# Layer 1's keys and queries: token sums behind the root, scaling by VectorE from one slot, values behind their pair, weight sums last

## The chip, the cores and the metric

One core of one Trainium2 chip runs the whole program in a single launch. TensorE (PE in the profile, PEld for its weight loads) does the matrix products, VectorE (DVE), ScalarE (ACT) and GpSimd (POOL) the elementwise work, SyncE (SP) and POOL issue most transfers. The metric is the device time of one execution in microseconds. A change of less than 0.2% (2.4 us) can't be told from no change here.

## The reference, cut to what matters

Two layers over 512 tokens of width 1024, in float32. Layer 0 has two kinds of dense attention, layer 1 has a neighbourhood attention with 16 heads of 64 columns. Each layer ends in a squared-ReLU MLP. The change touches layer 1's attention only.

```
def rmsnorm(x, g):
    y = xf * lax.rsqrt(jnp.mean(xf * xf, axis=-1, keepdims=True) + EPS)
    return (y * g.astype(jnp.float32)).astype(x.dtype)

def neighbourhood_attention(h, w_qkv, rpb, w_out):
    q, k, v = jnp.split(h @ w_qkv, 3, axis=-1)
    ...
        kg = jnp.take(k, iblk, axis=2)
        vg = jnp.take(v, iblk, axis=2)
        bias = rpb[:, rblk, cblk].astype(jnp.float32)
        sc = jnp.einsum('bhqd,bhqkd->bhqk', qblk, kg).astype(jnp.float32) * scale + bias[None]
        p = jax.nn.softmax(sc, axis=-1).astype(vg.dtype)
        return jnp.einsum('bhqk,bhqkd->bhqd', p, vg)
    ...
    return o @ w_out

for layer in range(DEPTH):
    hn = rmsnorm(h, norm_mix[layer])
    ...
        h = h + neighbourhood_attention(hn, od_w_qkv[i], od_rpb[i], od_w_out[i])
    h = h + sq_relu_mlp(rmsnorm(h, norm_ffn[layer]), ffn_w_up[layer], ffn_w_down[layer])
```

## The kernel before

**Numbers in two parts.** Every float32 operand of a product is split into a high part (ACT rounds it to fp32r) and a low part (DVE takes the difference). A product is three matmuls: high by high, high by low, low by high. `whi` and `wlo` are the parts of a weight chunk; `a` names the 8 KB slots that hold tokens, keys, queries and values, `sc` scratch tiles, `mm`, `s`, `t` and `o` the eight banks of PSUM (products, scores, transposes, outputs).

**The root.** The norm's factor of a token is the reciprocal root of its sum of squares. PE sums the squares (L661), DVE takes the mean and, in ten small operations, the root (L663, L186 to L196), and copies it to `r` (L1635). PE spreads it over 128 partitions (L669, a broadcast and transpose), ACT puts it into `rb` (L1641). The products run on tokens without the factor; it is multiplied in when keys and queries are evacuated from PSUM, and for values by L1863 and L1864.

**Keys and queries in pairs of heads.** Eight pairs, t = 0 to 7. `projC(t)` is the plain form: 48 matmuls of 128x128 by 128x512, keys first, then queries. The key's evacuation (L1687) and the query's (L1720, two pieces with a factor 0.125) multiply by `rb` on DVE. `projC7(t)`, for t = 1 to 5, is a seven-block form: the 2x2 blocks of weights and tokens are combined so that seven products do for eight, 84 matmuls of 128x128 by 128x256. It needs sums of weight blocks and of token blocks. `seven_pair` loads a chunk of weights and lets POOL make its sums (L390 to L392), then splits it (L396, L397). `SevenC.sums(kp)` makes the token sums for chunk pair kp = 0 to 3: ACT scales two chunks (L1661), POOL combines them (L1664 to L1666), ACT and DVE split the results (L1671, L1672). Four banks take a pair's products. `ev` combines them: ACT copies a half bank (L1771), DVE adds in four operations (L1774 to L1780), POOL multiplies by `rb` in five (L1781 to L1786), ACT and DVE split. The parts must also lie in the other half of the partitions: two transfers by POOL's queue (L1810, L1811) and, behind L1811's landing, one by SP's (L1815) for a query.

**The attention.** `attend_C` goes through 16 heads in two half-steps each: scores (L1898, four matmuls), DVE's bias and minimum (L1913), transposes of the head before (L1924), the exponential (L1932), the normalisation by POOL (L1902), and the output of the head before that (L1944). Between them the queue `fill` runs matmuls of projections not done yet: before this change, for t = 1 to 7, `projC7(t)` or `projC(t)`, with the values of four heads (`valuesC`, L1845 to L1847) put ahead of pairs 2, 4 and 6, and from head 12 on a part of the output projection. `RATE_C` sets how much is run at each place; `fill.until` makes a head wait until its pair was issued.

**What sets the order.** Inside the attention PE, ACT, DVE and POOL issue in the order in which the code is written (`fixed_order`); SP's is scheduled. Work that could hold up an engine is not written at once: `soon` puts it into the list `off_d`, `soon_a` into `off_a`, and `catch_up` takes it at fixed places. `banks_for` releases the PSUM layout and opens another: in `psC` five banks for products and one each for s, t and o, in `psD` three, two, two and one. Ahead of the attention a scheduler orders the instructions, except those that are pinned by `keep_in_program_order`.

## Time and profile before

| | us |
|---|---|
| runs | 1199.89, 1200.42, 1202.01; median 1200.42 |
| profiled execution | 1200.05, of which span 1198.30 |
| PE, DVE, ACT, POOL busy | 1150.9 (96%), 928.8 (78%), 688.5 (57%), 669.4 (56%) |
| before the attention's stage | to 600 |
| layer 1's attention with its opening | 600 to 842 |
| output projection's rest, MLP, final norm | 842 to 1198.3 |

The page's first part gives busy times. Since PE is nearly always busy, the views to read are those of its waits: by cause (`PE s L1898 <- DMA a<-sc` is PE's scores at line 1898 waiting for a transfer from scratch into a slot), by stretch (the windows, with the clock that PE was granted, 1.00 being full speed), and the timeline of an engine, where a bracket gives the idle time before an instruction and what ended it.

### The profile page before, as it was taken

Reading aid. Unit: us, or ns where it says so; the run is one execution under the profiler, and the core shown is the slowest. Engines: PE = TensorE matmul, PEld = TensorE weight load, DVE = VectorE, ACT = ScalarE, POOL = GpSimd, SP = SyncE. Lnnn points to the kernel's source line nnn. Section 1 sums busy time; section 2 is a strip of 40 time slices with the busy share of each in tenths; the row PEclk is TensorE's granted clock in tenths of the full one; section 3 lists DMA queues with packets and bytes.
Section 4 is the critical chain, followed back from the end, with each engine's and each line's share of the span. In section 5 each row is a group of like instructions: output and inputs, shape, how many; then the busy total and the mean of one; then the engine's idle time right before and its main releaser. Section 6 shows DMA issues by size and latency. Waiting matters only on the chain. (4 is left out here: it accounts for less than half of the span.)

```text
span 1198.3 us, 21112 instructions
## 1 busy us (share of the span) xinstructions
PE 1150.9 (96%) x7528; PEld 1037.1 (87%) x7528; DVE 928.8 (78%) x1593; ACT 688.5 (57%) x1164; POOL 669.4 (56%) x819
## 2 busy tenths in 40 slices
PE   9999999999999999999959797998999999999997
PEld 8787888888899998999949797877888999989996
DVE  7888998798778879787786765765798788688884
ACT  6576875656266677344745554644562566774434
POOL 4366422237888862697657854320087888626640
PEclk9999999999999999999979899999999999999999
DMA  7322441123422329434824535543335233182332
GB/s 228 106 82 69 106 124 54 47 95 117 153 76 87 106 69 264 156 106 128 155 70 111 147 109 142 136 120 114 97 98 166 72 93 102 56 196 67 116 130 71
DMA packets 118329, 136.10 MB, mean 114 GB/s; under 512 B 9923, under 2 KB 99952, under 8 KB 118224
## 3 DMA queue, kind: packets, MB, share of 16 engines
q1 hardware_dynamic: 110736, 119.83, 33.2%
q0 software_dynamic: 7312, 14.83, 6.6%
q8 instruction: 59, 0.97, 0.3%
q14 instruction: 46, 0.38, 0.1%
q10 hardware_dynamic: 176, 0.10, 0.0%
HBM read 112.70 MB, written 6.29 MB: 99 GB/s over the span
## 5 line engine op out<-in xcount | busy, mean ns | idle before, releaser
L376 DVE TENSOR_TENSOR wlo<-a,whi 128x896 fp32r<-128x896 f32 x106 | 132.6, 1253 | 56.7 <-ACT whi L375 56.2
L375 ACT ACTIVATE whi<-a 128x896 fp32r<-128x896 f32 x106 | 100.8, 951 | 111.6 <-PE o L479 28.6
L478 PE MATMUL mm<-a,whi 128*128 128x256 f32 x570 | 161.7, 284 | 2.8 <-DVE sc L1720 1.6
L480 PE MATMUL mm<-a,wlo 128*128 128x256 f32 x570 | 160.2, 281 | 4.1 <-DVE wlo L397 4.0
L479 PE MATMUL mm<-a,whi 128*128 128x256 f32 x570 | 159.8, 280 | 0.0
L640 PE MATMUL mm<-a,whi 128*128 128x512 f32 x348 | 142.8, 411 | 1.7 <-DVE sc L1117 1.7
L642 PE MATMUL mm<-a,wlo 128*128 128x512 f32 x348 | 138.5, 399 | 1.7 <-DVE wlo L229 1.7
L641 PE MATMUL mm<-a,whi 128*128 128x512 f32 x348 | 138.6, 398 | 0.0
L229 DVE TENSOR_TENSOR wlo<-raw,whi 128x1024 fp32r<-128x1024 f32 (+4 forms) x83 | 93.9, 1137 | 31.2 <-ACT whi L239 30.9
L239 ACT ACTIVATE whi<-raw 128x1024 fp32r<-128x1024 f32 (+3 forms) x86 | 77.4, 903 | 59.6 <-PE s L641 30.1
L480 PEld LDWEIGHTS mm<-a,wlo 128*128 128x128 f32 x570 | 107.5, 189 | 4.8 <-DVE wlo L397 4.7
L478 PEld LDWEIGHTS mm<-a,whi 128*128 128x128 f32 x570 | 107.6, 189 | 4.0 <-ACT whi L396 2.0
L479 PEld LDWEIGHTS mm<-a,whi 128*128 128x128 f32 x570 | 107.6, 189 | 0.1
L371 POOL TENSOR_TENSOR a<-a 128x128 f32<-128x128 f32 x104 | 100.9, 970 | 8.2
L375 ACT ACTIVATE whi<-raw 128x896 fp32r<-128x896 f32 x58 | 55.2, 954 | 83.7 <-POOL raw L371 24.9
L1173 POOL TENSOR_SCALAR p<-p,ti 128x512 f32<-128x512 f32 x64 | 47.3, 740 | 89.9 <-DVE ti L1172 66.6
L370 POOL TENSOR_TENSOR a<-a 128x256 f32<-128x256 f32 x104 | 92.5, 890 | 8.2
L376 DVE TENSOR_TENSOR wlo<-raw,whi 128x896 fp32r<-128x896 f32 x58 | 72.1, 1258 | 21.6 <-ACT whi L375 21.5
L478 PE MATMUL t<-a,whi 128*128 128x256 f32 x312 | 87.5, 281 | 0.0
L480 PE MATMUL t<-a,wlo 128*128 128x256 f32 x312 | 87.4, 280 | 0.0
L479 PE MATMUL t<-a,whi 128*128 128x256 f32 x312 | 87.3, 280 | 0.0
L369 POOL TENSOR_TENSOR a<-a 128x128 f32<-128x128 f32 x104 | 66.1, 636 | 34.5 <-DMA a<-in_ffn_w_up_dram 20.4
(477 smaller groups left out, 3688.2 us busy)
## 6 DMA issues: line engine op xcount, KB each, us to landing
a<-in_ffn_w_up_dram SPq DMA_DIRECT2D x102, 256.0 KB, 2.7
raw<-in_ffn_w_down_dram SPq DMA_DIRECT2D x34, 512.0 KB, 4.2
raw<-in_ffn_w_down_dram SPq DMA_DIRECT2D x56, 256.0 KB, 2.6
raw<-in_od_w_qkv_dram SPq DMA_DIRECT2D x64, 128.0 KB, 2.7
raw<-in_ffn_w_up_dram SPq DMA_DIRECT2D x12, 512.0 KB, 4.2
wlo<-in_ffn_w_down_dram POOLq DMA_DIRECT2D x12, 512.0 KB, 6.2
a<-a SPq DMA_DIRECT2D x17, 256.0 KB, 3.2
bx<-a SPq DMA_DIRECT2D x32, 128.0 KB, 5.4
```

The lines of the kernel that those rows point to most:

```text
L229: z = lambda: (eng or DVE).tensor_tensor(to, src, f32(high), op=ALU.subtract)
L239: ACT.activation(hi[:, 0:m], raw[:, 0:m], AF.Copy)
L370: held(eng.tensor_tensor(r[:, 4:6], r[:, 2:3].to_broadcast([P, 2, P]), r[:, 0:7:6], op=ALU.add))
L371: held(eng.tensor_tensor(r[:, 7], r[:, 3], r[:, 5], op=ALU.subtract))
L375: ACT.activation(hi[:, 0:896], raw[:, 128:1024], AF.Copy)
L376: DVE.tensor_tensor(lo[:, 0:896], raw[:, 128:1024], f32(hi[:, 0:896]), op=ALU.subtract)
L478: PE.matmul(o, wh, x[:, 0], start=kp == 0 and n in (0, 1, 3, 5), stop=False, skip_group_check=True)
L479: PE.matmul(o, wh, x[:, 1], start=False, stop=False, skip_group_check=True)
L480: PE.matmul(o, wl, x[:, 0], start=False, stop=kp == self.np - 1, skip_group_check=True)
L640: PE.matmul(o, wh, xh, start=first, stop=False)
L641: PE.matmul(o, wh, xl, start=False, stop=False)
L642: PE.matmul(o, wl, xh, start=False, stop=last)
```

## The change

1. The token sums were written between pair 0's products; now they are written behind them, all four in turn, and their first ACT operations (L1661) are pinned.
2. Pair 1 takes the plain form; the seven-block form is left for pairs 2 to 5.
3. `ev` of the seven-block form works in one slot instead of three scratches, and DVE does the scaling: one multiplication for keys, two with 0.125 for queries, in place of POOL's five.
4. POOL's weight sums of a chunk go into a list of their own, taken behind the normalisations of a half-step, or when the chunk is needed.
5. The values stand behind pairs 2, 4 and 6 in `fill` and no longer ahead of them.
6. The `psD` layout is opened inside the attention, by an entry of `fill` behind pair 5, and not after it.
7. `RATE_C` goes from 1.26 to 1.28.

```diff
--- before.py
+++ after.py
@@ -323,7 +323,7 @@
 
 
 
-    off_d, off_a = [], []
+    off_d, off_a, off_p = [], [], []
 
     def soon(z, later=None):
         if fixed[0]:
@@ -387,10 +387,16 @@
                          src[:, 0:2, P * t : P * t + P])
         r = raw.rearrange("p (b n) -> p b n", n=P)
         yield
-        POOL.tensor_tensor(r[:, 6], r[:, 0], r[:, 1], op=ALU.subtract)
-        POOL.tensor_tensor(r[:, 4:6], r[:, 2:3].to_broadcast([P, 2, P]), r[:, 0:7:6], op=ALU.add)
-        POOL.tensor_tensor(r[:, 7], r[:, 3], r[:, 5], op=ALU.subtract)
+
+        def sums():
+            POOL.tensor_tensor(r[:, 6], r[:, 0], r[:, 1], op=ALU.subtract)
+            POOL.tensor_tensor(r[:, 4:6], r[:, 2:3].to_broadcast([P, 2, P]), r[:, 0:7:6], op=ALU.add)
+            POOL.tensor_tensor(r[:, 7], r[:, 3], r[:, 5], op=ALU.subtract)
+
+        soon(sums, off_p)
         yield
+        while sums in off_p:
+            off_p.pop(0)()
         hi = wp.tile([P, 1024], F32R, tag="whi", name=nm("whi"))
         lo = wp.tile([P, 1024], F32R, tag="wlo", bufs=4, name=nm("wlo"))
         ACT.activation(hi[:, 0:896], raw[:, 128:1024], AF.Copy)
@@ -1658,7 +1664,8 @@
 
             raw, t = Slot(F32), scratch()
             for z in range(2):
-                ACT.activation(raw.t[:, S * z : S * z + S], hT[:, 2 * kp + z, :], AF.Copy, scale=gmix(1, 2 * kp + z))
+                tc.keep_in_program_order(ACT.activation(raw.t[:, S * z : S * z + S], hT[:, 2 * kp + z, :], AF.Copy,
+                                                        scale=gmix(1, 2 * kp + z)))
             yield
             r, t_ = (x.rearrange("p (b n) -> p b n", n=256) for x in (raw.t, t))
             POOL.tensor_tensor(t_, r[:, 0:1].to_broadcast([P, 2, 256]), r[:, 1:3], op=ALU.subtract)
@@ -1765,25 +1772,26 @@
 
         def ev(bk, half):
             d = PC[t]
-            X, Y, nq, nk = (scratch() for _ in range(4))
+            w_, rb = Slot(F32), hold["rb"]
+            n_, nk = scratch(), scratch()
+            r = w_.t.rearrange("p (b n) -> p b n", n=256)
             two = lambda b: b.rearrange("p (b n) -> p b n", n=256)
-            rb = hold["rb"]
-            ACT.activation(Y[:, 0:256], half(bk[0], 0), AF.Copy)
+            ACT.activation(r[:, 1], half(bk[0], 0), AF.Copy)
 
             def first():
-                DVE.tensor_tensor(two(X), two(Y)[:, 0:1].to_broadcast([P, 2, 256]), two(bk[1]), op=ALU.add)
-                DVE.tensor_tensor(two(Y), two(X)[:, 0:1].to_broadcast([P, 2, 256]), two(bk[2]), op=ALU.add)
+                DVE.tensor_tensor(r[:, 0:4:3], r[:, 1:2].to_broadcast([P, 2, 256]), two(bk[1]), op=ALU.add)
+                DVE.tensor_tensor(r[:, 1:3], r[:, 0:1].to_broadcast([P, 2, 256]), two(bk[2]), op=ALU.add)
                 soon(second)
 
             def second():
-                DVE.tensor_tensor(X[:, 0:256], Y[:, 0:256], half(bk[2], 1), op=ALU.add)
-                DVE.tensor_tensor(Y, Y, bk[3], op=ALU.add)
-                POOL.tensor_tensor(nk[:, 0:256], Y[:, 256:512], rb[:, 0:256], op=ALU.mult)
-                POOL.tensor_tensor(nk[:, 256:512], X[:, 256:512], rb[:, 256:512], op=ALU.mult)
+                DVE.tensor_tensor(r[:, 0], r[:, 1], half(bk[2], 1), op=ALU.add)
+                DVE.tensor_tensor(r[:, 1:3], r[:, 1:3], two(bk[3]), op=ALU.add)
+                DVE.tensor_tensor(nk, w_.t[:, S : 2 * S], rb, op=ALU.mult)
                 soon_a(lambda: split(nk, ka, down))
-                POOL.tensor_tensor(nq[:, 64:320], X[:, 0:256], rb[:, 0:256], op=ALU.mult)
-                POOL.tensor_tensor(nq[:, 320:512], Y[:, 0:192], rb[:, 256:448], op=ALU.mult)
-                POOL.tensor_tensor(nq[:, 0:64], Y[:, 192:256], rb[:, 448:512], op=ALU.mult)
+                for to, fr, m in ((64, 0, 448), (0, 448, 64)):
+                    DVE.scalar_tensor_tensor(n_[:, to : to + m], w_.t[:, fr : fr + m], 0.125, rb[:, fr : fr + m],
+                                             op0=ALU.mult, op1=ALU.mult)
+                w_.free()
                 soon_a(high)
 
             d["K"] = [Slot(), Slot()]
@@ -1802,11 +1810,11 @@
             lo = scratch(F32R)
 
             def high():
-                ACT.activation(q[:, 0, :], nq, AF.Copy, scale=0.125)
+                ACT.activation(q[:, 0, :], n_, AF.Copy)
                 soon(low)
 
             def low():
-                DVE.scalar_tensor_tensor(lo, nq, 0.125, f32(q[:, 0, :]), op0=ALU.mult, op1=ALU.subtract)
+                DVE.tensor_tensor(lo, n_, f32(q[:, 0, :]), op=ALU.subtract)
                 POOL.dma_start(f32(q[0:64, 1, :]), f32(q[64:128, 0, :]))
                 POOL.dma_start(f32(q[64:128, 1, :]), f32(lo[64:128, :]))
                 soon(last)
@@ -1961,6 +1969,7 @@
             for x in w:
                 norm(*x)
             catch_up()
+            take_up(off_p)
             fill.run(us)
             catch_up()
 
@@ -2012,25 +2021,29 @@
     next(root)
     for _ in first:
         pass
-    parts = [xC.sums(kp) for kp in range(4)]
     for n, _ in enumerate(second):
         if n == 2:
             next(root)
-        if n % 2 == 1:
-            for kp in range(4):
-                if kp <= n // 2 < kp + 3:
-                    next(parts[kp])
-    for x in parts:
-        for _ in x:
+    for kp in range(4):
+        for _ in xC.sums(kp):
             pass
+
+    def new_banks(name, **bufs):
+        finish_off()
+        banks_for(name, **bufs)
+        return
+        yield
+
     for t in range(1, 8):
+        fill.add(f"c{t}", projC7(t) if 2 <= t < 6 else projC(t))
+        if t == 5:
+            fill.add("c5", new_banks("psD", mm=3, s=2, t=2, o=1))
         if t in (2, 4, 6):
-            fill.add(f"c{t}", valuesC(t // 2, lambda: [mmb(), mmb()]))
-        fill.add(f"c{t}", projC7(t) if t < 6 else projC(t))
+            fill.add(f"v{t}", valuesC(t // 2, lambda: [mmb(), mmb()]))
     w_out1 = ins["od_w_out"][0]
     okC = [None] * 5
     rest = [out_proj(w_out1, 0, okC, cols, "out") for cols in ([0, 1, 2], [3, 4, 5], [6, 7])]
-    LEAD, RATE_C = 11.0, 1.26
+    LEAD, RATE_C = 11.0, 1.28
 
     def step(n):
         if n == 14:
@@ -2050,7 +2063,6 @@
         attend_C(step)
         give_low(len(ready))
         fixed[0] = 0
-    banks_for("psD", mm=3, s=2, t=2, o=1)
     ok = [s_.pair() for s_ in O[5:]]
     flip[0] = 1
     for c in range(2):
```

The order of the instructions shows what that does. Lines of the changed kernel are 6 to 8 higher for the same code (L1661 is L1667 there, L1671 is L1678, L1672 is L1679, L1687 is L1694).

ACT at the opening, before: the token sums (`a<-hT,gT` is the scaling of a chunk) stand ahead of the values' scaling by the root, L1863.

```order
L1661 ACTIVATE a_7153<-hT,gT 128x512
L1671 ACTIVATE a_7163<-sc_7134 128x2x256
L1671 ACTIVATE a_7166<-a_7133 128x2x256
L1661 ACTIVATE a_7172<-hT,gT 128x512 x2
L1671 ACTIVATE a_7182<-sc_7154 128x2x256
L1671 ACTIVATE a_7185<-a_7153 128x2x256
L1661 ACTIVATE a_7191<-hT,gT 128x512 x2
L1671 ACTIVATE a_7211<-sc_7173 128x2x256
L1671 ACTIVATE a_7214<-a_7172 128x2x256
L396 ACTIVATE whi_7279<-raw_7251 128x896
L1863 ACTIVATE a_7093<-o_6944,r_7061 128x4x64
```

The same place after: L1737 and L1738 are the split of pair 0's query (L1730 and L1731 before), and each chunk pair's scaling stands behind the split of the one before it.

```order
L1737 ACTIVATE sc_7184<-sc_7180 64x512
L1738 ACTIVATE a_7183<-sc_7180 64x512
L1667 ACTIVATE a_7191<-hT,gT 128x512 x2
L1678 ACTIVATE a_7198<-sc_7192 128x2x256
L1678 ACTIVATE a_7201<-a_7191 128x2x256
L1667 ACTIVATE a_7204<-hT,gT 128x512 x2
L402 ACTIVATE whi_7318<-raw_7265 128x896
L1678 ACTIVATE a_7211<-sc_7205 128x2x256
L1678 ACTIVATE a_7214<-a_7204 128x2x256
L1667 ACTIVATE a_7217<-hT,gT 128x512 x2
```

The sums moved from ahead of the root to behind pair 0's query, and the scaling no longer runs one chunk pair ahead.

DVE after, in the third and fourth chunk pair's sums (L1679): L1921 is the first head's scores, L1694 and L1727 pair 1's key and query.

```order
L1679 TENSOR_TENSOR a_7224<-sc_7218,a_7224 128x2x256
L1679 TENSOR_TENSOR a_7227<-a_7217,a_7227 128x2x256
L1921 ISA p_7360,ti_7365<-s_7359,bias_7357 128x256
L1921 ISA ti_7365 128x1
L1921 ISA p_7360,ti_7367<-s_7359,bias_7357 128x256
L1921 ISA ti_7367 128x1
L1694 TENSOR_TENSOR sc_7334<-mm_7248,rb 128x512
L1727 SCALAR_TENSOR_TENSOR sc_7371<-mm_7247,rb 128x448
L1727 SCALAR_TENSOR_TENSOR sc_7371<-mm_7247,rb 128x64
L1679 TENSOR_TENSOR a_7237<-sc_7231,a_7237 128x2x256
```

Before, all these sums stood ahead of the first scores; now the scores and pair 1's evacuation stand behind three of the four.

PE where pair 5's products end, before: the values of heads 12 to 15 (L1845) follow.

```order
L478 MATMUL mm_8526<-a_7229,whi_8600 128x256
L479 MATMUL mm_8526<-a_7229,whi_8600 128x256
L480 MATMUL mm_8526<-a_7229,wlo_8601 128x256
L1845 MATMUL mm_8767<-whi_8676,a_6919 128x256
L1846 MATMUL mm_8767<-wlo_8677,a_6919 128x256
```

After, pair 6's products (L646) follow, in a bank of the new layout.

```order
L484 MATMUL mm_8472<-a_7240,whi_8544 128x256
L485 MATMUL mm_8472<-a_7240,whi_8544 128x256
L486 MATMUL mm_8472<-a_7240,wlo_8545 128x256
L646 MATMUL mm_8709<-a_6919,whi_8598 128x512
L647 MATMUL mm_8709<-a_6919,whi_8598 128x512
```

The values moved behind pair 6, and the change of layout lies between the third and the fourth of these rows.

## The prediction

> **What bounds the kernel now.** Page first: TensorE is busy for 96% of the span, so only its waits and its slow clock can be won. The windows view shows where they lie (columns: busy time, with instructions, of PE, PEld, DVE, ACT and POOL, then the granted clock, DMA share and GB/s):
>
> ```profile
> 600.00:622.50 22.50, 9.86 (x36) 7.43 (x34) 19.70 (x30) 11.76 (x21) 12.96 (x15) 0.70 0.15 47
> 622.50:842.00 219.50, 194.65 (x1332) 179.28 (x1332) 141.92 (x354) 113.65 (x258) 103.03 (x169) 0.96 0.47 125
> 842.00:1198.30 356.30, 348.28 (x2363) 320.51 (x2361) 278.98 (x376) 192.75 (x272) 204.21 (x241) 1.00 0.36 106
> 613.60:618.20 4.60, 4.58 (x13) 3.77 (x14) 3.72 (x6) 3.53 (x7) 0.00 (x0) 0.52 0.38 114
> 684.00:688.60 4.60, 4.25 (x20) 4.28 (x21) 2.75 (x7) 2.28 (x6) 4.35 (x8) 0.50 0.30 70
> 736.80:741.00 4.20, 4.19 (x22) 4.19 (x23) 2.79 (x7) 2.59 (x7) 0.00 (x0) 0.59 0.76 213
> 829.50:842.00 12.50, 10.46 (x35) 8.54 (x36) 5.78 (x8) 2.29 (x3) 0.00 (x0) 0.73 0.46 147
> ```
>
> Layer 1's attention (600 to 842 us) has nearly all the loss that the change can reach. PE's waits there, one row for each cause (total, times, longest):
>
> ```profile
> PE t L669 <- DVE r L1635: 12.6, 1, 12.6
> PE s L1898 <- DMA a<-sc: 11.5, 3, 5.5
> PE mm L480 <- DVE wlo L397: 4.0, 2, 2.9
> PE mm L642 <- DVE wlo L229: 1.7, 1, 1.7
> PE mm L640 <- DVE sc L1117: 1.7, 1, 1.7
> PE t L1924 <- POOL p L1902: 1.7, 1, 1.7
> ```
>
> After 842 us PE has no wait for another engine, and from the next norm on both kernels have the same order on every engine. What the attention gains or loses therefore goes straight to the end.
>
> **The root.** The timeline shows why PE stands at 600.98 us (columns: start, length, engine, line, operation, and the idle time before it with its releaser):
>
> ```profile
> 594.68 0.95 PE L661 MATMUL t<-ones,acc 128*128 128x1 f32 x8
> 598.56 3.98 DVE L1672 TENSOR_TENSOR a<-sc,a 128x512 fp32r<-128x512 f32 x1 [5.57 <-ACT a L1671]
> 604.72 0.15 DVE L663 TENSOR_SCALAR ti<-t 128x4 f32<-128x4 f32 x1
> 613.62 1.11 PE L669 MATMUL t<-cst,r 128*128 128x128 f32 x4 [12.64 <-DVE r L1635]
> 862.63 0.16 DVE L663 TENSOR_SCALAR ti<-t 128x4 f32<-128x4 f32 x1
> 865.09 0.16 DVE L196 SCALAR_TENSOR_TENSOR ti<-ti,ti 128x4 f32<-128x4 f32 x1
> ```
>
> The squares' sums are there at 595.63, but the root starts at 604.72, behind the token sums in DVE's queue, and lasts until PE goes on at 613.62, 8.9 us among them. The same chain alone took 2.6 us from 862.63 to 865.25; with the copy of the root that follows it I count 2.8. The change puts the eight L1672 (and their ACT and POOL parts) behind the root. Then it ends at 598.4 if undisturbed, or at 602.6 if POOL's weight sums, which still run there, stretch it to 7 (between 2.8 and 8.9). PE is ready at 600.98: the wait is 0 to 1.6, and I take 0.8. That saves 11.8. The slow clock after the old wait (0.52 over 4.60 us, 4.60 x 0.48 = 2.2) goes too, and 0.6 of a 1.58 us wait behind it. **Root: -14.6.**
>
> **Pair 1 plain.** It becomes 48 matmuls with 512 columns instead of 84 with 256.
>
> ```profile
> 618.22 0.40 PE L640 MATMUL mm<-a,whi 128*128 128x512 f32 x1
> 622.18 0.40 PE L642 MATMUL mm<-a,wlo 128*128 128x512 f32 x1
> 624.16 0.35 PE L478 MATMUL mm<-a,whi 128*128 128x256 f32 x1 [1.58 <-DVE sc L1720]
> 634.08 0.28 PE L1845 MATMUL mm<-whi,a 128*128 128x256 f32 x1
> 624.04 0.63 ACT L1730 ACTIVATE sc<-sc 64x512 fp32r<-64x512 f32 x1 [0.70 <-DVE sc L1720]
> ```
>
> Seventeen steps from 618.22 to 622.18 give 0.233 each, and 84 from 624.16 to 634.08 give 0.118: 11.2 against 9.9. **Pair 1: +1.3.**
>
> **Token sums, now late.** Their rows (shortest/median/longest ns, first and last start):
>
> ```profile
> L1661 ACT ACTIVATE a<-hT,gT x8: 704/712/733, 576.8 to 605.4; 128x512 f32<-128x512 f32 x8
> L1664 POOL TENSOR_TENSOR sc<-a x4: 1259/1650/1804, 596.1 to 609.3; 128x512 f32<-128x512 f32 x4
> L1665 POOL TENSOR_TENSOR a<-a,sc x4: 717/1046/1127, 597.9 to 611.2; 128x256 f32<-128x256 f32 x4
> L1666 POOL TENSOR_TENSOR a<-a x4: 728/874/1054, 599.3 to 612.4; 128x256 f32<-128x256 f32 x4
> L1671 ACT ACTIVATE a<-a x4: 631/632/634, 600.4 to 621.9; 128x512 fp32r<-128x512 f32 x4
> L1672 DVE TENSOR_TENSOR a<-sc,a x4: 679/944/3981, 598.6 to 620.4; 128x512 fp32r<-128x512 f32 x4
> ```
>
> In the new ACT order each chunk pair's L1661 stands behind the L1671 of the one before, so the four cycles run in series: two L1661 (start to start 0.66, 1.3 together), POOL 2.70 to 3.98 (I take 3.1, near the lowest since less runs beside it), one L1671 0.63, hand-overs 0.3: 5.3 each. The first stands behind pair 0's query pieces L1730 and L1731. L1730 began 1.6 after pair 0's last matmul (622.41 to 624.04), and the two take 1.3, so counted from that matmul's end, sums start at 2.9 and three cycles end at 18.8. VectorE's order then has the third cycle's L1672 (0.6), two pieces of scores (0.9) and pair 1's key evacuation (0.6): 20.9. PE meanwhile waits 1.0 for the evacuation of pair 0, does pair 1 (11.2), the first scores (0.5) and 15 matmuls of pair 2 (1.8), and then needs the bank which that evacuation frees: 14.5. A new wait of 6.4. Behind it the weights of pair 2's third and fourth chunk pairs are split late, since ACT's and VectorE's parts stand behind the fourth cycle: by the same counting 0.9, 2.2, 1.3 and 0.9, 5.3 in all. Clock: 2.3 was lost after the 5.5 us wait (0.50 over 4.60 us); I take 2.5. **Opening: +14.2**, with bounds of 8 (POOL at its shortest, no clock loss) and 20 (POOL at 4.0 in each of three cycles, +2.7, and slow clock after the lesser waits too, +3).
>
> The Trainium skill, "TensorE: Matmul & The Clock Gate", section "What's actually happening", has the clock halve only after an idle window of about 3.4 us. The trace agrees after 5.5 us (0.50), but 829.50 to 842 has 0.73 with no single wait above 1.75. By that rule the lesser waits would cost no clock and the opening would be about 13.5.
>
> **The transfers.** Scores waited three times for the last part of a pair's query. For pair 2:
>
> ```profile
> 662.64 0.37 ACT L1771 ACTIVATE sc<-mm 128x256 f32<-128x256 f32 x1
> 665.62 0.69 DVE L1780 TENSOR_TENSOR sc<-sc,mm 128x512 f32<-128x512 f32 x1
> 669.02 0.34 POOL L1786 TENSOR_TENSOR sc<-sc,rb 128x64 f32<-128x64 f32 x1
> 672.63 0.69 DVE L1809 SCALAR_TENSOR_TENSOR sc<-sc,a 128x512 fp32r<-128x512 f32 x1
> 674.87 0.53 POOL L1811 DMA_DIRECT2D a<-sc  x1
> 679.10 0.52 SPq L1815 DMA_DIRECT2D a<-sc  x1
> 684.35 1.19 PE L1898 MATMUL s<-a,a 128*128 128x256 f32 x4 [5.54 <-DMA a<-sc]
> ```
>
> The chain is 21.7 us long, two transfers in series at its end. Against it stands PE's work between a pair's last product and its first scores. I added it up from PE's order, with the steps above and 0.47, 0.44 and 0.9 for a half-step's scores, transposes and values: 12.9, 11.9 and 9.7 us for pairs 2, 4, 6, which waited, and 13.9 to 20.6 for pairs 1, 3, 5, 7, which did not. With each pair ahead of its values it becomes 27.2, 26.5 and 24.5 for pairs 2, 4, 6 and 18.3, 19.4, 19.3, 15.5 for the odd ones. The scaling by VectorE replaces POOL's part, from the end of L1780 (666.31) to 669.36, by three operations (0.69, 0.62 and 0.22 by the rows under the next heading), and adds 1.5 to VectorE: about a microsecond shorter. So the 11.5 of waits goes, with the clock behind two of them (2.3, and 4.20 x 0.41 = 1.7); I leave 0.8. **Transfers: -14.7.**
>
> **Weights, banks, end.** Groups of evacuations in 622 to 842 us (count, busy time, mean ns of one):
>
> ```profile
> L1687 DVE TENSOR_TENSOR sc<-mm,rb 128x512 f32<-128x512 f32 x2 | 1.4, 692 | 1.1 <-PE mm L642 1.1
> L1720 DVE SCALAR_TENSOR_TENSOR sc<-mm,rb 128x448 f32<-128x448 f32 x3 | 1.8, 616 | 0.0
> L1720 DVE SCALAR_TENSOR_TENSOR sc<-mm,rb 128x64 f32<-128x64 f32 x3 | 0.6, 215 | 0.0
> ```
>
> The weight waits on L397 (4.0) came from places in the order that no longer exist; I leave 0.8: -3.2. The normalised scores p now go ahead of POOL's weight sums, so the 1.7 us wait for POOL goes: -1.7. If they still wait, both terms are zero.
>
> Opening the other bank layout behind pair 5 makes pair 6's first product wait for pair 5's last evacuation, the L1774 to L1780 group: L1771 to the end of L1780 is 3.7 above; 3.6 taken, between 2.9 (no queue) and 4.5 (a half-step's operations ahead of it), with 1.0 of clock (0 to 1.7): +4.6. In exchange the end of the attention has two transpose banks and the next projection's first products ahead of the last values: the waits 1.7 (L1117), 1.7 (L229) and 0.4 and the slow clock of 829.50 to 842 (12.50 x 0.27 = 3.4) go but for 0.5: -6.7. Short bank waits in pairs 3 and 4, where VectorE has some 14.4 to 15.7 us of work for 13.2 of PE's: +2.4, between 0 and 5.
>
> **Sum:** -14.6 + 1.3 + 14.2 - 14.7 - 3.2 - 1.7 + 4.6 - 6.7 + 2.4 = -18.4. The profiled execution took 1200.05 us, 1.75 around its span and 0.37 under the runs' median of 1200.42: about 1181.6.
>
> **Rivals.** (1) **The opening takes back more.** The sums run as slowly as before, when one L1672 took 3.98 and POOL's part 3.9, or the root is still stretched beyond 602.6 by weight sums. Either adds 6 to 8: 1188. For it: those rows; against: fewer operations now run beside each other. (2) **The opening takes back little.** POOL's part stays near 2.7, PE's later waits merge into the first, and no clock is lost: opening +7 instead of +14.2, and the bank switch 2 less: 1173. For it: the last chunk pair's neighbours were light; against: the series in ACT's order. (3) **VectorE becomes the bound**, the other side. Each seven-block pair brings it 1.5 more, 6.1 for four pairs, while its chain of evacuation, scaling and split queues behind half-steps. Average load speaks against this (141.92 + 6 of 219.50 less about 19). It decides where VectorE's delay makes the chain (about 20.7) longer than the odd pairs' 19.3 by more than the slack that they showed before: each further microsecond is a wait. With 6 us at pairs 3, 4, 5 and 6 (24), their clock (4 x 2 = 8), less 0.8 already counted: 1181.6 + 31 = 1213, slower. The point is 4.6 us a pair, where the gain of 18.4 is gone. The Trainium skill, "GPSIMD Engine Reference", section "1. Specifications", says that POOL shares its SBUF interfaces with VectorE, contended by VectorE operations with two SBUF inputs. The three new operations are of that kind, and the 3.98 us L1672 beside POOL's L390 and L1665 agrees with it. (4) That the change does not do what it says is excluded for the root by the order: L1672 stands behind L1635 on VectorE.
>
> **How the numbers follow.** Forecast (1176 to 1187): 0.54. Rival 1 (1187 to 1194): 0.20. Rival 2 (under 1176): 0.15. Rival 3: 0.06, all of it above 1202.8. The remaining 0.05 is for partial mishaps between 1194 and 1203, 0.04 of it within 0.2%. A difference of 0.2% (2.4 us) is about what a measurement of this kernel tells from no change. So faster 0.90, same 0.04, slower 0.06. The range 1172 to 1192 takes the bounds of the opening (-6, +6) with those of the root, the bank switch and VectorE's load, and leaves out some 0.15.
>
> **What would show it.** Right: one root wait under 2 us at L669; a new PE wait of 5 to 8 us inside pair 2, released by VectorE's L1694 (new L1687); no scores waiting for a query's transfer; a 3 to 4 us wait at pair 6's first product. Wrong: scores of pairs 3 to 6 released by DMA or VectorE, or the opening's waits above 15 us.

## The result

The changed kernel takes 1182.76 us in the median of four runs (1182.45 to 1183.57), the kernel before 1200.16 beside it. The ratio is 0.9855 with a 95% interval of 0.9838 to 0.9873: 1.5% faster, 17.4 us. The forecast was 1181.6 in a range of 1172 to 1192. The profiled execution took 1182.45, its span 1180.7.

### The profile after

The windows over the whole stretch between two common points, from the root's sums of squares (L661, now L667) to those of the next norm, of before and after (columns as in the prediction: busy time of PE, PEld, DVE, ACT, POOL, then the granted clock):

```profile
594.68:860.75 266.07, 228.57 (x1488) 207.04 (x1487) 180.81 (x410) 140.03 (x299) 121.28 (x189) 0.94 0.43 113
```

```profile
594.99:843.55 248.56, 227.40 (x1453) 204.99 (x1451) 177.59 (x419) 140.86 (x300) 101.89 (x158) 0.96 0.44 119
```

All of the 17.5 us lies here (266.07 against 248.56; the spans differ by 17.6). PE's idle time went from 37.5 to 21.2 us, so the waits gave 16.3. Its busy time fell by 1.2 although pair 1's plain form adds about 1.3 of work, so slow clock gave some 2.5. Read from the granted clock itself, in windows of a quarter of a microsecond, it gave 1.2 (9.9 us lost before, 8.7 after). What follows this stretch has the same length within 0.4 us.

PE's waits for other engines in the changed kernel, from 595 to 830 us (total, times, longest), which answer to the six rows shown of before:

```profile
PE mm L484 <- DVE sc L1694: 5.2, 1, 5.2
PE t L1932 <- POOL p L1910: 4.9, 4, 2.7
PE mm L646 <- DVE a L1788: 3.7, 1, 3.7
PE mm L646 <- DVE sc L1727: 2.9, 2, 2.3
PE mm L484 <- ACT whi L402: 2.2, 1, 2.2
PE mm L484 <- ACT a L1779: 1.2, 1, 1.2
PE mm L486 <- DVE wlo L403: 0.9, 2, 0.6
```

The root (12.6) and the three waits of scores for transfers (11.5) are gone, and so are the waits at the attention's end (L1117, L229). New are pair 1's key evacuation (L1694), the weights' split behind it (L402), and the bank of pair 6 (L1788). One row of before has grown: the transposes' wait for the normalised scores, from 1.7 to 4.9.

The windows from the opening on:

```profile
613.00:640.00 27.00, 21.18 (x112) 18.58 (x110) 12.52 (x25) 12.45 (x22) 17.94 (x21) 0.84 0.29 76
640.00:660.00 20.00, 17.55 (x123) 17.26 (x124) 14.50 (x36) 10.98 (x26) 9.92 (x17) 0.83 0.46 117
720.00:740.00 20.00, 16.33 (x106) 15.00 (x105) 15.32 (x36) 10.16 (x23) 6.12 (x10) 0.91 0.55 154
740.00:822.00 82.00, 81.14 (x493) 71.13 (x492) 55.62 (x150) 45.08 (x108) 20.79 (x37) 1.00 0.42 127
```

The mean clock of a window counts idle time too. In windows of a quarter of a microsecond the granted clock is 0.50 from 611.4 to 614.8 (on pair 1's products, behind a wait of 2.29 us for pair 0's bank), from 628.4 to 635.3 (around the wait of 5.16), from 642.1 to 648.9 (around the waits of 2.20 and 0.33) and from 730.8 to 734.3 (around the wait of 3.67 for pair 6's bank), and 1.00 between them. On PE's busy time in these stretches half speed costs 1.7, 2.3, 3.2 and 1.5 us. So the opening loses clock three times, most of it where the longest wait is only 2.20. The end of the attention, 0.73 before, has full speed.

The chain of the opening, from the timelines of ACT, POOL, DVE and PE in the changed kernel:

```profile
611.36 1.32 ACT L1667 ACTIVATE a<-hT,gT 128x512 f32<-128x512 f32 x2
616.72 0.63 ACT L1678 ACTIVATE a<-a 128x512 fp32r<-128x512 f32 x1 [1.35 <-POOL a L1673]
618.65 1.32 POOL L1671 TENSOR_TENSOR sc<-a 128x512 f32<-128x512 f32 x1 [1.97 <-ACT a L1667]
624.63 1.28 POOL L1671 TENSOR_TENSOR sc<-a 128x512 f32<-128x512 f32 x1 [1.97 <-ACT a L1667]
629.84 1.28 POOL L1671 TENSOR_TENSOR sc<-a 128x512 f32<-128x512 f32 x1 [1.96 <-ACT a L1667]
628.58 0.69 DVE L1679 TENSOR_TENSOR a<-a,a 128x512 fp32r<-128x512 f32 x1 [1.27 <-ACT a L1678]
629.18 0.42 DVE L1921 CUSTOM_DVE_ANT_0 p<-s,bias 128x256 f32<-128x256 f32 x1
629.87 0.69 DVE L1694 TENSOR_TENSOR sc<-mm,rb 128x512 f32<-128x512 f32 x1
630.61 0.58 PE L484 MATMUL mm<-a,whi 128*128 128x256 f32 x1 [5.16 <-DVE sc L1694]
```

The cycles run in series, 5.98 and 5.21 us from one L1671 to the next (5.3 was reckoned). POOL is idle for 2 us in each, waiting for ACT's scaling, which stands behind ACT's split of the cycle before. The key evacuation begins 22 us after pair 0's last product ends (607.8), 20.3 by the reckoning.

### The profile page after: what moved, and what is told of

It reads as the page before. It is cut to its first block, busy times and chain, and to the rows that moved or that the text cites. A ratio compares the mean times of both kernels' runs of the same rounds, so it can differ in the third digit from the quotient of the medians.

```text
span 1180.7 us, 20992 instructions
## 1 busy us (share of the span) xinstructions
PE 1150.0 (97%) x7492; PEld 1035.1 (88%) x7492; DVE 923.3 (78%) x1602; ACT 686.4 (58%) x1161; POOL 644.4 (55%) x782
## 4 chain that ended last, share of the span: by engine, by line
PE 83%; DVE 6%; issue 5%; POOL 3%; ACT 2%; DMA 0%; POOLq 0%; DVEq 0%; ACTq 0%
PE mm L646 7%; PE mm L648 7%; PE mm L647 7%; PE mm L486 5%; PE mm L484 4%; PE mm L485 4%; PE t L484 3%; PE t L486 3%; PE t L485 3%; PE s L1171 3%; PE o L1159 2%; PE s L646 2%; PE s L648 2%; PE s L647 2%; PE s L484 2%
## 5 line engine op out<-in xcount | busy, mean ns | idle before, releaser
L484 PE MATMUL mm<-a,whi 128*128 128x256 f32 x542 | 155.1, 286 | 8.5 <-DVE sc L1694 5.2
L646 PE MATMUL mm<-a,whi 128*128 128x512 f32 x364 | 148.8, 409 | 6.7 <-DVE a L1788 3.7
L486 PE MATMUL mm<-a,wlo 128*128 128x256 f32 x542 | 153.7, 283 | 0.9 <-DVE wlo L403 0.9
L485 PE MATMUL mm<-a,whi 128*128 128x256 f32 x542 | 153.4, 283 | 0.0
L647 PE MATMUL mm<-a,whi 128*128 128x512 f32 x364 | 144.6, 397 | 0.0
L648 PE MATMUL mm<-a,wlo 128*128 128x512 f32 x364 | 144.3, 398 | 0.0
L229 DVE TENSOR_TENSOR wlo<-raw,whi 128x1024 fp32r<-128x1024 f32 (+4 forms) x85 | 96.6, 1141 | 25.2 <-ACT whi L239 24.8
L484 PEld LDWEIGHTS mm<-a,whi 128*128 128x128 f32 x542 | 103.9, 192 | 9.2 <-DVE sc L1694 5.4
L371 POOL TENSOR_TENSOR a<-a 128x128 f32<-128x128 f32 x104 | 103.6, 996 | 8.2
L486 PEld LDWEIGHTS mm<-a,wlo 128*128 128x128 f32 x542 | 103.8, 192 | 1.6 <-DVE wlo L403 1.6
L485 PEld LDWEIGHTS mm<-a,whi 128*128 128x128 f32 x542 | 104.0, 192 | 0.1
L370 POOL TENSOR_TENSOR a<-a 128x256 f32<-128x256 f32 x104 | 90.0, 865 | 8.2
L646 PEld LDWEIGHTS mm<-a,whi 128*128 128x128 f32 x364 | 69.0, 190 | 21.3 <-issue 7.6
```

Of the source, the lines that this page charges most:

```text
L229: z = lambda: (eng or DVE).tensor_tensor(to, src, f32(high), op=ALU.subtract)
L370: held(eng.tensor_tensor(r[:, 4:6], r[:, 2:3].to_broadcast([P, 2, P]), r[:, 0:7:6], op=ALU.add))
L371: held(eng.tensor_tensor(r[:, 7], r[:, 3], r[:, 5], op=ALU.subtract))
L484: PE.matmul(o, wh, x[:, 0], start=kp == 0 and n in (0, 1, 3, 5), stop=False, skip_group_check=True)
L485: PE.matmul(o, wh, x[:, 1], start=False, stop=False, skip_group_check=True)
L486: PE.matmul(o, wl, x[:, 0], start=False, stop=kp == self.np - 1, skip_group_check=True)
```

## The experiments

The theory on record was that each part is worth the wait it removes, less the wait it makes: above all that the root's gain is paid back in the opening, and that the work between a pair's products and its scores is what hides the transfers. The rivals were VectorE as the bound, and gains that come from another part. Times are medians; ratios are to the kernel before on the same chip. "Theory A" and "Rival B" are those of the expectation quoted in each section. No run takes `RATE_C` back alone, so what it gives is not shown. Pair 1's form was varied only with the token sums in front.

### One part undone: the token sums in front

```diff
+    parts = [xC.sums(kp) for kp in range(4)]
     for n, _ in enumerate(second):
         if n == 2:
             next(root)
-    for kp in range(4):
-        for _ in xC.sums(kp):
+        if n % 2 == 1:
+            for kp in range(4):
+                if kp <= n // 2 < kp + 3:
+                    next(parts[kp])
+    for x in parts:
+        for _ in x:
             pass
```

L1667 isn't pinned here.

> The changed kernel with one part undone: the token sums are written between pair 0's products as before, the rest stays (pair 1 plain, values behind, layout behind pair 5). In the changed kernel the root has no wait, but the opening has 8.3 us of new waits (5.16 + 2.20 + 0.58 + 0.33) and granted clocks of 0.84 and 0.83 over 613 to 660, some 6 us. Theory A (the root's gain is paid back in the opening): the wait at L675 returns with about 12 us and 2 us of clock, the waits in pair 2 go, and the time is within 3 us of the changed kernel's 1182.8, so 1180 to 1186. Rival B (the sums behind the root are where the gain comes from): 1193 to 1197, with the root's wait back and the opening's not smaller.

1186.44 us, ratio 0.988 (0.9858 to 0.9902), 3.7 above the changed kernel. The waits:

```profile
PE t L675 <- DVE r L1641: 11.0, 1, 11.0
PE t L1931 <- POOL p L1909: 6.2, 4, 2.7
PE mm L646 <- DVE sc L1726: 4.8, 2, 4.2
```

The root waits 11.0 again, and the waits inside pair 2 are gone but for 0.45. Theory A holds in kind; the time is just above its 1186. The part is worth 3 to 4 us and not 14: most of what it takes from the root it gives back in the opening. Between the two norms PE idles 27.57 us here and 21.16 in the changed kernel, but is busy for 224.88 against 227.40: with the sums in front less clock is lost.

### The first two parts undone

The token sums in front as in the run above, and:

```diff
-        fill.add(f"c{t}", projC7(t) if 2 <= t < 6 else projC(t))
+        fill.add(f"c{t}", projC7(t) if t < 6 else projC(t))
```

> The changed kernel without its first two parts: token sums between pair 0's products and pair 1 seven-block, all the rest as changed. Theory A (with the sums in front, pair 1's plain form only costs its 1.3 us and the longer bank wait of 4.18 against 1.58): 1182 to 1185, so that the first two parts together are worth next to nothing in the changed kernel. Rival B (the seven-block pair 1 makes its own evacuation and scaling late for the first scores and lengthens the waits behind it): 1187 to 1191.

1184.34 us, ratio 0.9852 (0.9835 to 0.9868): the changed kernel's own 0.9855 within the intervals. This is Theory A. The token sums and the plain pair 1 together gave nothing that can be told from zero, and the 17.4 us come from the other parts. The two times agree by different sums, however: between the two norms PE idles 25.70 us here, 4.5 more than in the changed kernel, and is busy for 222.83, 4.6 less. Of the 4.6 only about 1.1 is pair 1's work; the rest is clock. Of that 1.7 was lost behind the wait for pair 0's bank in the changed kernel and nothing here, though that wait is 3.66 us long. Against the run above, which differs only in pair 1, the plain form costs 2.1 us (3.4 by the ratios).

### One part undone: values ahead

```diff
+        if t in (2, 4, 6):
+            fill.add(f"c{t}", valuesC(t // 2, lambda: [mmb(), mmb()]))
         fill.add(f"c{t}", projC7(t) if 2 <= t < 6 else projC(t))
...
-        if t in (2, 4, 6):
-            fill.add(f"v{t}", valuesC(t // 2, lambda: [mmb(), mmb()]))
```

> The changed kernel with one part undone: the values of four heads stand again ahead of pairs 2, 4 and 6. Theory A (the work between a pair's last product and its first scores hides the query's transfers): the waits of scores for transfers return at pairs 2, 4 and 6 with 9 to 13 us in all and a clock of one half behind at least two of them; 1192 to 1198. Rival B (the faster chain by VectorE's scaling and one slot already did it): at most 3 us of such waits, 1182 to 1186.

1195.55 us, ratio 0.9959 (0.9944 to 0.9974), 12.8 above. The waits of its scores:

```profile
PE s L1906 <- DMA a<-sc: 12.2, 3, 6.1
PE s L1906 <- DVE ti L1921: 4.8, 2, 4.6
```

Three waits for transfers are back, 12.2 us against 11.5 before, at pairs 2, 4 and 6. Theory A: VectorE's shorter chain alone hides none of it. The 4.8 is another effect of this order, the opening's wait at another place (629 us).

### This part alone, on the kernel before

```diff
-        if t in (2, 4, 6):
-            fill.add(f"c{t}", valuesC(t // 2, lambda: [mmb(), mmb()]))
         fill.add(f"c{t}", projC7(t) if t < 6 else projC(t))
+        if t in (2, 4, 6):
+            fill.add(f"v{t}", valuesC(t // 2, lambda: [mmb(), mmb()]))
```

> The kernel before with one part of the change alone: the values stand behind pairs 2, 4 and 6. Theory A (this part is the largest; undoing it alone in the changed kernel cost 12.8 us): the 11.5 us of scores waiting for transfers and some 4 us of clock go, and new waits of transposes for normalised scores (7.2 us where POOL did the scaling, against 1.7 before) take back 3 to 6: 1187 to 1192. Rival B (without VectorE's shorter chain the odd pairs' scores now wait, since their work of 19.4 us is less than the chain's 21.7): two or three waits of 2 us or more, 1194 to 1200.

1195.45 us, ratio 0.9941 (0.9922 to 0.9959): 6.4 below the kernel before on this chip. By its time this is Rival B, by its mechanism it is not, since no scores wait for a transfer, of the odd pairs either. The waits:

```profile
PE t L669 <- DVE r L1635: 10.7, 1, 10.7
PE t L1924 <- POOL p L1902: 5.4, 2, 3.2
PE s L1898 <- DVE ti L1913: 4.5, 2, 3.4
PE t L1924 <- DVE a L1927: 2.5, 2, 2.1
```

The 11.5 us went, and so did the 4.0 for split weights (0.2 left). But the waits of scores and transposes for VectorE and POOL are now 12.4 us, where they were 2.7 (1.7 for POOL, 1.0 for VectorE): 9.7 came back. Both theories missed the size. The next run makes POOL's scaling a likely part of it; for the waits on VectorE's L1913 no run took the cause apart.

### One part undone: scaling by POOL

```diff
-                DVE.tensor_tensor(nk, w_.t[:, S : 2 * S], rb, op=ALU.mult)
...
-                    DVE.scalar_tensor_tensor(n_[:, to : to + m], w_.t[:, fr : fr + m], 0.125, rb[:, fr : fr + m],
-                                             op0=ALU.mult, op1=ALU.mult)
+                POOL.tensor_tensor(nk[:, 0:256], Y[:, 256:512], rb[:, 0:256], op=ALU.mult)
+                POOL.tensor_tensor(nk[:, 256:512], X[:, 256:512], rb[:, 256:512], op=ALU.mult)
...
+                POOL.tensor_tensor(nq[:, 64:320], X[:, 0:256], rb[:, 0:256], op=ALU.mult)
+                POOL.tensor_tensor(nq[:, 320:512], Y[:, 0:192], rb[:, 256:448], op=ALU.mult)
+                POOL.tensor_tensor(nq[:, 0:64], Y[:, 192:256], rb[:, 448:512], op=ALU.mult)
```

ScalarE's factor of 0.125 and the three scratches in place of one slot are back too; the diff above leaves these lines out.

> The changed kernel with one part undone: the scaling by the root is done by POOL in five operations from three scratches, as before. Theory A (VectorE's load made the four waits of transposes for the normalised scores, 4.9 us, because the reciprocals stand behind the pair's evacuation and scaling in its queue): these waits fall to under 2 us, no scores wait for a transfer since 24 us of work cover a chain of 22; 1179 to 1182. Rival B (POOL's queue then makes them late, since five operations of 0.6 to 0.7 stand ahead of the normalisation): the same or more waits on POOL, 1183 to 1187. If scores of the odd pairs (19.4 us of work) wait for transfers by 2 us each: 1187 to 1190.

1189.04 us, ratio 0.9899 (0.9878 to 0.9921), 6.3 above. Theory A falls: the waits for normalised scores grow from 4.9 to 7.2 and do not shrink. Rival B had the direction, but expected no more than 4 us. POOL's timeline around the longest of them:

```profile
706.94 0.73 POOL L1788 TENSOR_TENSOR sc<-sc,rb 128x256 f32<-128x256 f32 x1 [4.28 <-DVE ti L1908]
707.63 0.72 POOL L1789 TENSOR_TENSOR sc<-sc,rb 128x256 f32<-128x256 f32 x1
708.31 0.72 POOL L1791 TENSOR_TENSOR sc<-sc,rb 128x256 f32<-128x256 f32 x1
709.00 0.59 POOL L1792 TENSOR_TENSOR sc<-sc,rb 128x192 f32<-128x192 f32 x1
709.55 0.77 POOL L1793 TENSOR_TENSOR sc<-sc,rb 128x64 f32<-128x64 f32 x1
710.30 0.93 POOL L1909 TENSOR_SCALAR p<-p,ti 128x256 f32<-128x256 f32 x2
```

Five scalings, 3.4 us, stand directly ahead of the normalisation (L1909) for which PE waits until 710.83. In the changed kernel VectorE does the same in 1.3 us (701.65 to 702.93 on its timeline). PE's idle time between the two norms is 26.8 us here and 21.2 in the changed kernel. The part is worth 6 by POOL's and VectorE's queues, and not by the transfers' chain, to which the prediction put it down: no scores wait for a transfer here either.

### One part undone: the second PSUM layout at the end

```diff
-        if t == 5:
-            fill.add("c5", new_banks("psD", mm=3, s=2, t=2, o=1))
...
         fixed[0] = 0
+    banks_for("psD", mm=3, s=2, t=2, o=1)
```

> The changed kernel with one part undone: the second PSUM layout is opened after the attention. Theory A (the forecast's two terms): the wait of 3.67 us at pair 6's first product goes with some 1.5 us of clock, and the attention's end gets back waits of about 3.9 us and 3.4 us of clock: 1183 to 1187, 2 us above the changed kernel. Rival B (the end's waits came from the old order of values and are gone anyway): 1177 to 1179.

1184.64 us, ratio 0.9861 (0.984 to 0.9882), 1.9 above, at the edge of what can be told. The 3.67 us at pair 6 go (720 to 760 us has a clock of 1.00), and the end gets waits of 1.43, 1.97 and 1.40 and a clock of 0.96 in 760 to 850. Both terms of Theory A are there.

### One part undone: weight sums at once

```diff
-        soon(sums, off_p)
+        sums()
```

> The changed kernel with one part undone: POOL makes a chunk's weight sums as soon as the chunk is planned, ahead of the normalisations, as before. Theory A (the forecast's term): the waits of transposes for normalised scores grow from 4.9 us by 1 to 3, the waits for split weights stay under 2: 1184 to 1187. Rival B (the sums come earlier, so the weights of the opening, 2.20 and 0.33 us of waits at 642 us, are there in time): 1179 to 1182.

1176.56 us, ratio 0.9795 (0.9776 to 0.9815): 6.2 below the changed kernel. This part of the change is a loss, as Rival B says, and a larger one. PE's waits of this run from 613 to 700 us (timeline), then two of its windows:

```profile
632.22 0.58 PE L484 MATMUL mm<-a,whi 128*128 128x256 f32 x1 [7.69 <-DVE sc L1694]
639.02 0.39 PE L486 MATMUL mm<-a,wlo 128*128 128x256 f32 x1 [0.66 <-DVE wlo L403]
...
698.74 0.47 PE L1932 MATMUL t<-cst,p 128*128 128x128 f32 x1 [3.03 <-POOL p L1910]
```

```profile
613.00:640.00 27.00, 18.65 (x101) 16.48 (x100) 13.64 (x27) 14.26 (x27) 17.70 (x20) 0.87 0.30 72
640.00:660.00 20.00, 20.00 (x173) 20.00 (x173) 17.59 (x45) 13.62 (x33) 15.88 (x26) 1.00 0.76 186
```

The opening waits as long as before, 8.35 us against 8.27, but in one piece and a remainder. The waits of 2.20 and 0.33 at 642 us are gone, where in the changed kernel ACT's split waited 5.46 us for a weight sum that POOL had put behind the normalisations. With them goes the slow clock around them (3.2 us). The waits for normalised scores are 3.0 instead of 4.9, though the sums no longer make way for them. Between the two norms PE idles 19.92 us (21.16 in the changed kernel) and is busy for 222.92 (227.40), so most of the 5.7 us gained there is clock (4.5 by the busy time, 3.6 by the granted clock). Of this, 1.7 is the fall behind pair 0's bank, which this run does not have after a longer wait (2.67 against 2.29); the last section shows why, and that much of the gain may be chance.

### Two chunk pairs of token sums ahead

```diff
-    for kp in range(4):
-        for _ in xC.sums(kp):
-            pass
+    parts = [xC.sums(kp) for kp in range(4)]
+    for kp in range(2):
+        next(parts[kp])
+    for kp in range(4):
+        next(parts[kp])
+        next(parts[kp])
+        if kp + 2 < 4:
+            next(parts[kp + 2])
```

> The changed kernel with the token sums behind the root, but two chunk pairs scaled by ScalarE before the first is split, so that GpSimd's part of one runs beside the scaling of the next (one more slot in use). Theory A (the opening waits because the four cycles run in series, 5.2 to 6.0 us each): three cycles become about 3 us each, the 5.16 us wait for pair 1's key evacuation falls to under 1, the 2.20 and 0.58 us waits to under 2 together, and most of the 5 us of slow clock goes: 1172 to 1177. Rival B (GpSimd's part is longer when it runs beside ScalarE's and VectorE's, as in the kernel before): 1179 to 1182.

1178.56 us, ratio 0.9815 (0.9794 to 0.9835), 4.2 below the changed kernel, a little better than Rival B and short of Theory A. The 5.16 us wait for L1694 is gone, but PE then stands for 4.47 us at the next chunk of weights (ACT's L402, 629.35 us), whose split stands behind the sums on ACT. Series on one engine was replaced by the queue on it.

### The scaling and POOL's part ahead of the root

```diff
+    parts = [xC.sums(kp) for kp in range(4)]
+    for kp in range(2):
+        next(parts[kp])
     next(root)
     for _ in first:
         pass
+    for kp in range(2):
+        next(parts[kp])
     for n, _ in enumerate(second):
         if n == 2:
             next(root)
-    for kp in range(4):
-        for _ in xC.sums(kp):
-            pass
+    for kp in range(2):
+        next(parts[kp])
+        if kp + 2 < 4:
+            next(parts[kp + 2])
+    for kp in range(2, 4):
+        next(parts[kp])
+        next(parts[kp])
```

The splits (L1678, L1679) are pinned too, so that none of them gets ahead of the root.

> The changed kernel with the scaling of the first two chunk pairs by ScalarE ahead of the root (it stood idle for 9.2 us there) and GpSimd's part right behind (it stood idle for 6.7 us from 600), while the splits, which hold VectorE, stay behind the root and are pinned. Theory A (what delayed the root was VectorE's queue, not the sums as such): the root's wait stays under 2 us, all sums are split by 621 and the opening has no wait over 1.5 us but that for pair 0's bank (2.29): 1169 to 1174. Rival B (GpSimd's sums beside the root stretch its small operations, as before, when the chain took 8.9 us instead of 2.6): a root wait of 3 to 6 us and the opening as in the run two chunk pairs ahead, 1175 to 1181.

1174.69 us, ratio 0.9783 (0.9759 to 0.9807), 8.1 below. VectorE's timeline at the root (its first and last operation), and the two longest of PE's waits up to 640 us:

```profile
596.17 0.16 DVE L669 TENSOR_SCALAR ti<-t 128x4 f32<-128x4 f32 x1 [3.85 <-PE t L667]
599.45 0.32 DVE L1641 COPY r<-ti 128x4 f32<-128x4 f32 x1
```

```profile
610.70 0.77 PE L646 MATMUL mm<-a,whi 128*128 128x512 f32 x1 [2.51 <-DVE sc L1727]
630.32 0.39 PE L486 MATMUL mm<-a,wlo 128*128 128x256 f32 x1 [0.68 <-DVE wlo L403]
```

The waits are Theory A's, but the last splits end at 623.5 and not 621, and the time lies 0.7 us above its range and just under Rival B's. The root takes 3.6 us and PE does not wait for it, although POOL works beside it. What had held it back was mostly the splits in VectorE's queue. With the rest of the sums early, the opening's 5.16 and 2.20 us are gone.

### Normalisation ahead of the deferred work

```diff
             fill.run(us)
+            for x in w:
+                norm(*x)
             catch_up()
             if ripe:
                 finish(ripe)
             fill.run(us)
-            for x in w:
-                norm(*x)
             catch_up()
```

> The changed kernel with the normalisations of a half-step taken ahead of the deferred work and not behind it, so that on VectorE the reciprocals stand ahead of a pair's evacuation and scaling. Theory A (the four waits for normalised scores, 4.9 us, come from the reciprocals' place in VectorE's queue): they fall to under 1.5 us and the time to 1178 to 1181. Rival B (VectorE's load as such: what is served first only makes the other late): the evacuations come later, PE waits for banks by as much, 1182 to 1186.

1190.26 us, ratio 0.991 (0.9889 to 0.9931), 7.5 above. The four waits for normalised scores are gone as Theory A says, and the time rises, as Rival B says and beyond it: the first bank behind a seven-block pair is waited for by 4.37 us (1.18 in the changed kernel, ACT's L1779), weights by 2.96 at 730 us, and the opening's waits grow to 6.72, 1.39, 2.17 and 1.71. Which work is served first only chooses who waits; the evacuations are the dearer ones.

### What beats both

The sums ahead of the root (as in that run) and the weight sums at once, together; and then the second layout opened behind pair 6 instead of pair 5 as well:

```diff
-        soon(sums, off_p)
+        sums()
...
-        if t == 5:
-            fill.add("c5", new_banks("psD", mm=3, s=2, t=2, o=1))
+        if t == 6:
+            fill.add("c6", new_banks("psD", mm=3, s=2, t=2, o=1))
```

> The changed kernel with two of the changes tried so far together: the first two chunk pairs of token sums scaled and combined ahead of the splits, and POOL's weight sums made as soon as the chunk is planned. If the two gains (8.1 and 6.2 us) are of different waits: 1168 to 1170. If both are mostly the same opening waits (5.16, 2.20, 0.58, 0.33 and their clock): 1172 to 1175, with the waits of transposes for normalised scores at 3 us instead of 5.5.

> The same two together, and the second PSUM layout opened behind pair 6 instead of pair 5. Pair 6 is plain and has only a two-piece evacuation behind its last product, against four operations and a copy behind pair 5's. Theory A: the 3.67 us wait becomes 1 to 2.3 us and its clock loss of 1.5 goes: 2 to 4 us below the run without it. Rival B (the attention's end needs the second layout earlier, and pair 6 and the values share too few banks): within 1 us or above.

Without the layout 1168.6 us, ratio 0.9723 (0.9707 to 0.9738): the two gains add up (8.1 and 6.2; together 14.2). PE's idle time between the two norms falls by 1.2 us with the weight sums at once, by 5.9 with the sums ahead of the root and by 7.7 with both, and its busy time by 4.5, 2.3 and 6.1: the gains were of different waits and clock. With it 1167.08, ratio 0.9707 (0.969 to 0.9724): 1.5 less, under the 2 expected, and the intervals overlap. The wait at the new layout is 1.34 in place of 3.67, but 0.76 came back at another normalisation and 0.70 at L1694. PE's longest waits left in this last one:

```profile
PE mm L646 <- DVE sc L1727: 3.8, 2, 3.2
PE t L1932 <- POOL p L1910: 3.7, 3, 2.8
PE mm L486 <- DVE wlo L403: 1.5, 1, 1.5
PE mm L1853 <- DVE sc L1727: 1.3, 1, 1.3
```

## Why the prediction was right

The time came within 1.2 us of the forecast, by terms that were partly wrong and cancelled; so close a number was luck. By its own sum, waits were to give 13.6 us and clock 6.1, against 1.3 of work; measured were 16.3 and 1.2 to 2.5.

- **Root (-14.6):** right as to the wait. PE reaches L675 at 601.12 without one, and pair 0 ends at 607.8 instead of 622.4. But the 0.6 that it took from the bank wait behind is wrong: that wait grew from 1.58 to 2.29. And of the 2.2 us of clock 1.7 was lost again behind that bank.
- **Opening (+14.2):** the mechanism was right to the instruction (the cycles in series on ACT, then pair 1's key evacuation behind the scores). The 11.7 of waits was 8.3. The clock behind the long wait was 2.3 for the 2.5 charged, but the waits of 2.20 and 0.33, charged with nothing, cost 3.2. The step that failed is this one: the clock was charged to the long wait alone. The two errors nearly cancel (13.8 in all).
- **Root and opening together:** the forecast had them, with pair 1, at +0.9. The run without both parts agrees in time: nothing, by waits and clock that cancel.
- **Transfers (-14.7):** the mechanism is right, shown from both sides. No scores wait, and with the values ahead 12.2 us are back. The lead in PE's work is the cause; VectorE's scaling isn't. The size depends on the rest: undoing this part costs 12.8 us, and alone on the kernel before it gives 6.4. The term's 2.3 of clock behind the 5.54 us wait was read from a window that ends too early: the slow stretch lasts from 682.9 to 689.7 and costs 2.7.
- **Weights (-3.2):** behind the opening no wait for L403 is left, so 4.0 less the 0.9 counted there. On the kernel before, the values' place alone takes these waits to 0.2 us, and with the weight sums at once they are 0.7, so they don't hang on the deferred sums.
- **Normalised scores (-1.7):** wrong in sign, +3.2. The term looked only at POOL's queue. On VectorE's timeline, ahead of the longest of the four waits, the reciprocals (L1909) stand behind the pair's evacuation and scaling:

```profile
700.93 0.69 DVE L1788 TENSOR_TENSOR a<-a,mm 128x512 f32<-128x512 f32 x1
701.65 0.69 DVE L1789 TENSOR_TENSOR sc<-a,rb 128x512 f32<-128x512 f32 x1
702.26 0.75 DVE L1792 SCALAR_TENSOR_TENSOR sc<-a,rb 128x448 f32<-128x448 f32 x2
702.93 0.21 DVE L1909 RECIPROCAL ti<-ti 128x1 f32<-128x1 f32 x2
```

  With the normalisations taken first, these waits are gone. This is Rival 3's queue, at a small price. And the deferred weight sums, to which the term was put down, cost 6.2 us, 1.7 of which may be chance: the whole part was misjudged.
- **Layout (+4.6, -6.7):** the wait is 3.67 (3.6 forecast), with 1.5 of clock; the end runs at full speed. Undone, the two nearly cancel, +1.9, as their difference said (2.1).
- **Small bank waits (+2.4):** in pairs 3 and 4 there is one, of 1.18 us, in pair 4. Another of 0.66 is in the output projection behind pair 7.
- **VectorE's scaling:** costed as a microsecond off a hidden chain, hence nothing. It is worth 6.3 us by way of POOL's queue. That the total still came out is because the loss by the weight sums was missed too.
- **Rival 3's example:** by the timelines the 3.98 us L1672 (from 598.56) ran beside POOL's L1665 and L391, but not L390, which ended at 598.27.

## What to carry to other kernels

A wait that is moved behind something is only gained if the new place has slack: here most of the 14 us won at the root were paid in the opening, and splitting the step into its cheap early half (scaling and sums) and its queue-blocking half (splits on VectorE) kept the gain. Undo each part of a change that won: one of seven was a loss, of 6 us by its run, inside a gain of 17. Look at every in-order queue on which a deferred operation then stands, not at the one it leaves.

## What the runs showed of the hardware

TensorE's clock does not follow the length of a single wait. Behind the wait for pair 0's bank, waits of 2.29 us (the changed kernel) and 2.51 us (the sums ahead of the root) were followed by a slow clock, and waits of 2.67 (the weight sums at once), 3.16 (the last kernel) and 3.66 (the first two parts undone) were not, with nearly the same work there.

The place of the idle time decides. In all 14 profiles the slow stretches around the attention have a clock of 0.50 and last 3.41 us or a multiple of it. Within a profile they begin whole multiples of 3.41 us apart: in the changed kernel the stretches from 628.44, 642.10 and 730.84 begin 5, 9 and 35 times 3.41 us behind the first, at 611.38. So the clock is set anew on a fixed grid of 3.41 us, and PE's idle time inside one piece of the grid goes with the clock of the next. In the changed kernel all of the 2.29 us falls into one piece (3.41 less 1.12 busy):

```profile
607.97:611.38 3.41, 1.12 (x6) 0.95 (x6) 3.32 (x6) 2.20 (x5) 2.20 (x4) 1.00 0.47 111
611.38:614.79 3.41, 3.41 (x10) 2.63 (x9) 1.16 (x2) 1.36 (x4) 2.08 (x4) 0.50 0.95 249
```

With the first two parts undone the 3.66 us are cut in two, 1.88 and 1.78, and the pieces behind have full speed:

```profile
619.63:623.04 3.41, 1.53 (x7) 0.91 (x5) 2.40 (x3) 2.91 (x5) 3.25 (x5) 1.00 0.03 8
623.04:626.45 3.41, 1.63 (x14) 1.66 (x15) 3.32 (x7) 1.60 (x3) 1.64 (x4) 1.00 0.61 153
626.45:629.86 3.41, 3.41 (x31) 3.41 (x30) 2.44 (x2) 0.95 (x1) 2.20 (x5) 1.00 0.66 159
```

The others fit: 2.19 us of idle time in one piece with the sums ahead of the root, and two pieces of 1.10 and 1.58 with the weight sums at once and of 1.65 and 1.52 in the last kernel. From about 590 to 845 us the 14 profiles have 939 such pieces at full speed, on a grid laid by each profile's first slow stretch. All 52 with 1.9 us or more of idle time were followed by 0.50, none of the 877 with less than 1.72, and 3 of the 10 between. What ends a slow stretch is less clear: the one from 642.10 lasted two pieces, though PE idled for only 0.35 us in the first.

The rule that was weighed in the prediction (the Trainium skill, "TensorE: Matmul & The Clock Gate", section "What's actually happening": a fall only after an idle window of about 3.4 us) would have no fall behind the waits of 2.29 and 2.51 us; there the measurement decides. The same section says that the window runs free, and the grid agrees with it.

For an estimate it means that a wait of 2 to 3.7 us can cost nothing, 1.7 us of clock (half of 3.41) or more (3.2 behind the 2.20), by where it falls, and that short gaps add up when they share a piece. Each profile shows one execution; where the grid lay in the others is not known. Differences of 1.7 us between two kernels can therefore be chance of this kind.
